# Attention scores from stacked query halves: one full-height and one half-height product in place of three half-height ones

## The chip, the cores and the metric

The kernel runs on one NeuronCore of a Trainium2 chip. Its time is the device time in microseconds (us) of one launch; a shorter time is better. The engines are TensorE (matmul), VectorE, ScalarE, GpSimd and SyncE, which issues most of the DMAs; GpSimd's queue issues some.

## What is computed

Two layers of a diffusion backbone work on 512 latent and 256 context tokens of width 1024. Each layer has a token mixer (a state-space part, a Fourier part and an attention part side by side) and a SwiGLU feed-forward part. The change is in the attention part, which has 6 heads of 64 dimensions:

```python
qg = q.reshape(B, R, GRID_W, H, d)          # 8 rows x 64 columns of latent tokens
s_win = einsum('bqhd,bwqkhd->bhqwk', q_row, k_win) * scale + bias   # 8 rows x 16 columns around
s_ctx = einsum('bqhd,bchd->bhqc', q_row, kc) * scale                # all 256 context keys
p = softmax(concatenate([s_win, s_ctx], -1))
o = p_win @ v_win + p_ctx @ vc
# na_context, in the first layer only: softmax(qc kc^T * scale) @ vc
```

## The kernel before

All matmuls keep float32 accuracy with a split: a value x is stored as hi, a rounded copy in the matmul's own 4-byte format (F32R), and lo = x - hi. A product of two such values is taken as hi*hi + hi*lo + lo*hi, three matmuls into the same PSUM tile.

Projection. `w_in` (the loop over column chunks, `CHUNKS`) makes queries and keys transposed, feature by token: chunk q0 holds heads 0 and 1, 64 rows each. `ev_q` and `ev_k` hand the chunk to `rope` (L686), which rotates it, splits it and stores hi and lo to DRAM on SyncE's queue (L708). The DRAM tensors `qd` and `kd` have for each of 384 feature rows first hi and then lo, 768 tokens each.

Attention. `attn` goes through three head pairs hp and, in each, through four latent query tiles of 128 tokens (`scores`) and in layer 0 one step for the context queries (`scores_ctx`): 15 steps in layer 0, 12 in layer 1, 27 in all. `attn_load` (L925) brings a pair's queries (L932, L937) and keys (L933) in on GpSimd's queue; the first two pairs are loaded ahead of the steps, the third during the second pair. The 128 partitions are 2 heads x 64 features. In each step `both` (L977) is called twice, for 256 window keys and for 256 context keys; a call makes for each head e three matmuls of 64 rows by 128 columns with 256 moving columns (L982): q_hi k_hi, q_hi k_lo, q_lo k_hi. Head 0 uses rows 0 to 63 of the array, head 1 rows 64 to 127, and the loop alternates the heads. Each head has a PSUM tile of 512 columns, from a pool "a" of two. VectorE then adds bias and mask and takes the row minimum (L1003), ScalarE takes the exponential, VectorE normalises (L1027), TensorE transposes the result (L1039) and multiplies by the values (L1054, and L1064 for context queries). Bias tiles come from `rbd`, which is filled by transfers of 6 x 16 rows of 1.5 KB (L923), and are combined with a mask on GpSimd (L994).

Fill. The steps are woven with other work: the Fourier part (L846, L856, L861), the gated unit (L819), and in layer 0 the modulation vectors (L161), whose weights are loaded at that time.

Order. `TileContext(schedule_with_timeline_sim=True)` is a planner that runs when the program is built. It orders each engine's instructions on its own estimate of when they become ready, so the order on TensorE need not be that of the loops. Once built, each engine works its list in order.

Pools that matter: `s` (24 buffers of 512 columns), `c` (22 of 256), `tab` (3 of 1536), `u` (one of 2816, holds the queries as `ua`).

Of the kernel before, what the change touches and what calls it, by code (L numbers as in the profile page):

```python
# [8 lines left out]
F32 = mybir.dt.float32  # L9
F32R = mybir.dt.float32r  # L10
# [8 lines left out]
NL, NC = 512, 256  # L19
NT = NL + NC  # L20
DEPTH = 2
NH, HD = 6, 64
# [12 lines left out]
class Builder:  # L35
# [60 lines left out]
    def consts(self):  # L96
        nc = self.nc
        self.cols = self.k("cols", [128, 8])
        nc.sync.dma_start(self.cols, self.ap["cols"])
        self.ident = self.k("ident", [128, 128])  # L100
        self.nidx = self.k("nidx", [128, 96])
        self.eye16 = self.k("eye16", [128, 16])
        self.junk = self.k("junk", [128, 512], mybir.dt.bfloat16)
        self.zero = self.k("zero", [1, 128], mybir.dt.bfloat16)
        nc.vector.memset(self.zero, 0.0)
        self.sgn, self.nsgn, self.sgn2pi, self.halfpi = (self.cols[:, i:i + 1] for i in range(4))
        self.mhalf = self.cols[:, 4:5]
        self.qd = [self.dram(f"qd{l}", [NH * HD, 2, NT]) for l in range(DEPTH)]
        self.kd = [self.dram(f"kd{l}", [NH * HD, 2, NT]) for l in range(DEPTH)]
        self.ud = [self.dram(f"ud{l}", [G, HC, 8, 128]) for l in range(DEPTH)]  # L110
        self.zd = [self.dram(f"zd{l}", [G, HC, 8, 96]) for l in range(DEPTH)]
        self.tabd = [self.dram(f"tabd{l}", [NU, 2, 128, 1792]) for l in range(DEPTH)]
        self.wd = [self.dram(f"wd{l}", [NU, 128, 240]) for l in range(DEPTH)]
        self.gd = [self.dram(f"gd{l}", [4, DM]) for l in range(DEPTH)]
        self.rbd = [self.dram(f"rbd{l}", [NH, 16, 8, 384]) for l in range(DEPTH)]
        self.xd = [self.dram(f"xd{l}", [6, 128, DM]) for l in range(3)]
        self.turn = [self.k(f"turn{l}", [128, 48]) for l in range(DEPTH)]
        self.rho = [self.k(f"rho{l}", [128, 48]) for l in range(DEPTH)]
        self.mcol = [[self.k(f"mc{l}{a}", [128, 2, 16]) for a in range(3)] for l in range(DEPTH)]
        self.gcol = [self.k(f"gcol{l}", [128, 2, 8]) for l in range(DEPTH)]  # L120
        self.amod = [[self.k(f"am{l}{i}", [128, 2, 8]) for i in range(2)] for l in range(DEPTH)]
        self.dcol = [self.k(f"dcol{l}", [128, NU]) for l in range(DEPTH)]
# [555 lines left out]
        self.fh[j], self.fl[j] = self.split2(eo, pc)  # L678

    def ev_q(self, l, j, pl, pc):  # L680
        self.rope(lambda i: self.qd[l][128 * j:128 * j + 128, i], pl, pc, -HD ** -0.5)

    def ev_k(self, l, j, pl, pc):
        self.rope(lambda i: self.kd[l][128 * j:128 * j + 128, i], pl, pc, 1.0)

    def rope(self, dst, pl, pc, scale):  # L686
        nc = self.nc
        if self.rc is None:
            self.rc, self.rs = self.s(), self.s()
            nc.sync.dma_start(self.rc, self.ap["rope"][:, 0, :])  # L690
            nc.sync.dma_start(self.rs, self.ap["rope"][:, 1, :])
        q, sh = self.s(), self.s()
        nc.scalar.activation(q, pl, AF.Copy, scale=scale)
        nc.vector.stream_shuffle(sh, q, [(i + 16) % 32 for i in range(32)])
        nc.gpsimd.tensor_tensor(out=sh, in0=sh, in1=self.rs, op=ALU.mult)
        self.tt(q, q, self.rc, ALU.mult)
        self.tt(q, q, sh, ALU.add)
        parts = [(q, 0, NL)]
        if pc is not None:
            qc = self.c()  # L700
            nc.scalar.activation(qc, pc, AF.Copy, scale=scale)
            parts.append((qc, NL, NT))
        for x, a, b in parts:
            new = self.s if a == 0 else self.c
            hl = (new(F32R), new(F32R))
            self.split(*hl, x)
            for i in range(2):
                nc.sync.dma_start(dst(i)[..., a:b], hl[i].bitcast(F32))  # L708


    def ssm_scan(self, l, k, tab):
# [212 lines left out]

    def attn_load(self, l, hp):  # L925

        nc = self.nc
        last = l == DEPTH - 1
        kt = self.tab(F32R, (128, 2, NT))
        rows = slice(128 * hp, 128 * hp + 128)  # L930
        ql = self.Q[hp % 2]
        nc.gpsimd.dma_start(ql, self.qd[l][rows, :, 0:NL])  # L932
        nc.gpsimd.dma_start(kt, self.kd[l][rows])  # L933
        qc = None
        if not last:
            qc = self.QC[hp % 2]
            nc.gpsimd.dma_start(qc, self.qd[l][rows, :, NL:NT])  # L937
        rb = self.z_p.tile([128, 2, 384], F32, tag="z", name="rb")
        for e in range(2):
            nc.sync.dma_start(rb[:, e, :], self.rbd[l][2 * hp + e].rearrange("c r n -> (c r) n"))  # L940
        return kt, ql, qc, rb
# [34 lines left out]

    def both(self, sp, q, k, qs, ks):  # L977

        for n, (a, b) in enumerate(((0, 0), (0, 1), (1, 0))):
            for e in range(2):  # L980
                r = slice(64 * e, 64 * e + 64)
                self.nc.tensor.matmul(sp[e], q[r, a, qs], k[r, b, ks], start=(n == 0), stop=(n == 2))  # L982

    def scores(self, l, hp, i):
        nc = self.nc
# [464 lines left out]
```

## Time and profile before

| | |
|---|---|
| median of 3 runs | 1678.88 us (1678.62 to 1682.22) |
| profiled execution | 1677.44 us |
| its span, first to last instruction | 1675.6 us |
| TensorE matmuls in flight | 1596.9 us (95%), 9097 matmuls |
| VectorE / ScalarE / GpSimd busy | 1037.3 / 608.9 / 378.8 us |
| mean granted TensorE clock | 0.977 of full speed |
| moved by DMA | 240.08 MB |

A row of the timeline merges like instructions that follow each other: start, busy time, engine, line, what is written from what, shape, count. "64*128 64x256" is a matmul that uses 64 rows and 128 columns of the array with 256 moving columns. A matmul's busy time includes its way through the array, and matmuls overlap; what one costs in a stream is the distance from its start to the next one's start. L982 is line 982 of the kernel.

### The profile page before, as it was taken

The page shows a single profiled execution, that of the slowest core. Times are in us where ns is not written, and L with a number is a line of the kernel's source. Part 1 is how long each engine was busy: PE and PEld are TensorE (multiplying, and loading weights), DVE is VectorE, ACT ScalarE, POOL GpSimd, SP SyncE. Part 2 cuts the span into 40 slices and gives each one's busy share as a digit, 9 for nine tenths or more (in the row PEclk, how much of TensorE's full clock was granted, in tenths as well). Part 3 has the DMA queues.
Part 4 walks back from the last instruction along what each step waited for, and adds up shares of the span by engine and source line. Part 5 has one row for each costly group of instructions (what it writes and reads, how often), then busy time and mean ns, then how long its engine had stood idle before and what let it go on. Part 6 is the DMA issues. An engine that isn't in the chain of part 4 may idle for free. (4 is left out here: it accounts for less than half of the span.)

```text
span 1675.6 us, 23600 instructions
## 1 busy us (share of the span) xinstructions
PE 1596.9 (95%) x9097; PEld 1311.2 (78%) x9097; DVE 1037.3 (62%) x1911; ACT 608.9 (36%) x1101; POOL 378.8 (23%) x384
## 2 busy tenths in 40 slices
PE   5988789999999999999999999999999999999997
PEld 1777676678898788878787788988778888888886
DVE  7799985774774667434434348698773634455455
ACT  5434344654627322112211127321563532222222
POOL 3367773100310323100000005276410100000002
PEclk8999799999999999999999999999899999999999
DMA  9343339662313334534423537367713322233222
GB/s 327 128 136 111 100 101 306 225 217 94 127 57 138 129 119 142 195 114 163 148 105 114 191 114 236 132 233 227 228 52 139 139 101 101 76 102 102 97 78 85
DMA packets 101391, 240.08 MB, mean 143 GB/s; under 512 B 25424, under 2 KB 56784, under 8 KB 88480
## 3 DMA queue, kind: packets, MB, share of 16 engines
q1 hardware_dynamic: 97968, 229.93, 40.3%
q0 software_dynamic: 3312, 8.65, 1.7%
q8 instruction: 71, 1.16, 0.3%
q14 instruction: 40, 0.33, 0.1%
HBM read 201.26 MB, written 38.47 MB: 143 GB/s over the span
## 5 line engine op out<-in xcount | busy, mean ns | idle before, releaser
L589 PE MATMUL b<-s,wh 128*128 128x512 f32 (+1 forms) x1856 | 553.6, 377 | 2.3 <-ACT s L580 0.8
L589 PEld LDWEIGHTS b<-s,wh 128*128 128x128 f32 x1856 | 339.9, 190 | 73.9 <-issue 10.6
L589 PE MATMUL b<-s,wl 128*128 128x512 f32 (+1 forms) x928 | 346.8, 375 | 2.5 <-DVE wl L561 2.5
L580 ACT ACTIVATE wh<-wr 128x1024 fp32r<-128x1024 f32 (+4 forms) x184 | 185.0, 1026 | 337.8 <-PE b L589 240.3
L561 DVE TENSOR_TENSOR wl<-wr,wh 128x1024 fp32r<-128x1024 f32 (+4 forms) x184 | 224.5, 1236 | 101.9 <-ACT wh L580 96.6
L278 DVE TENSOR_TENSOR q<-q,b 128x512 f32<-128x512 f32 (+1 forms) x192 | 129.2, 675 | 166.0 <-PE b L1178 165.3
L589 PEld LDWEIGHTS b<-s,wl 128*128 128x128 f32 x928 | 176.0, 190 | 33.2 <-DVE wl L561 3.8
L589 PE MATMUL b<-c,wh 128*128 128x256 f32 x944 | 183.8, 289 | 0.0
L589 PEld LDWEIGHTS b<-c,wh 128*128 128x128 f32 x944 | 154.7, 195 | 5.9 <-issue 0.6
L281 DVE SCALAR_TENSOR_TENSOR s<-s,b 128x512 f32<-128x512 f32 x88 | 60.2, 684 | 132.8 <-PE b L589 84.3
L1178 PE MATMUL b<-wh,tab 128*128 128x512 f32 x400 | 137.2, 393 | 0.1
L589 PE MATMUL b<-c,wl 128*128 128x256 f32 x472 | 134.9, 288 | 0.0
L1178 PE MATMUL b<-wh,s 128*128 128x512 f32 x384 | 129.5, 391 | 0.0
L1210 POOL TENSOR_TENSOR q<-q,g 128x512 f32<-128x512 f32 x10 | 13.8, 1380 | 361.2 <-ACT junk L515 335.5
L589 PEld LDWEIGHTS b<-c,wl 128*128 128x128 f32 x472 | 92.5, 196 | 1.7 <-issue 0.4
L1178 PEld LDWEIGHTS b<-wh,tab 128*128 128x128 f32 x400 | 75.1, 188 | 19.4 <-ACT c L1155 2.5
L1178 PEld LDWEIGHTS b<-wh,s 128*128 128x128 f32 x384 | 72.1, 188 | 19.9 <-ACT c L1155 2.5
L1178 PE MATMUL b<-wl,tab 128*128 128x512 f32 x200 | 78.3, 392 | 0.0
L1178 PE MATMUL b<-wl,s 128*128 128x512 f32 x192 | 74.6, 390 | 0.0
L527 POOL TENSOR_TENSOR ss<-ss,cols 128x1 f32<-128x1 f32 x42 | 31.0, 739 | 192.2 <-DVE ss L281 191.5
L580 ACT ACTIVATE s<-s 128x512 fp32r<-128x512 f32 x43 | 27.0, 627 | 122.0 <-DVE s L281 58.5
L452 POOL TENSOR_TENSOR u<-x,u 128x576 f32<-128x576 f32 x24 | 30.7, 1280 | 175.2 <-PE b L480 142.7
(311 smaller groups left out, 2735.8 us busy)
## 6 DMA issues: line engine op xcount, KB each, us to landing
wr<-in_w_gu SPq DMA_DIRECT2D x44, 1024.0 KB
wmod<-in_w_mod SPq DMA_DIRECT2D x46, 512.0 KB
wr<-in_w_down SPq DMA_DIRECT2D x22, 1024.0 KB
wmod<-in_w_mod SPq DMA_DIRECT2D x16, 1024.0 KB
wr<-in_w_in SPq DMA_DIRECT2D x10, 1024.0 KB
u<-in_w_mod SPq DMA_DIRECT2D x18, 512.0 KB
wr<-in_w_out SPq DMA_DIRECT2D x8, 1024.0 KB
tab<-tabd SPq DMA_DIRECT2D x12, 640.0 KB
```

What stands on the lines that cost most here:

```text
L278: self.nc.vector.tensor_tensor(out=out, in0=a, in1=b, op=op)
L281: self.nc.vector.scalar_tensor_tensor(out=out, in0=a, scalar=s, in1=b, op0=op0, op1=op1)
L452: g.tensor_tensor(out=cl, in0=v(2).unsqueeze(2).to_broadcast(sc), in1=clr.unsqueeze(3).to_broadcast(sc), op=ALU.mult)
L527: nc.gpsimd.tensor_tensor(out=ss[:, 3:4], in0=ss[:, 2:3], in1=self.mhalf, op=ALU.pow)
L561: (eng or self.nc.vector).tensor_tensor(out=lo, in0=x, in1=hi.bitcast(F32), op=ALU.subtract)
L580: ins = self.nc.scalar.activation(hi, x, AF.Copy)
L589: self.nc.tensor.matmul(out, a[k], h[k][v][:, cs], start=(k == 0 and i == 0), stop=(k == 7 and i == 2))
L1178: nc.tensor.matmul(pd, a[v][:, cs], w[:, ds], start=(j == 0 and i == 0), stop=(j == n - 1 and i == 2))
L1210: (nc.gpsimd, nc.vector)[hf].tensor_tensor(out=oo[hf], in0=oo[hf], in1=gates[t // 4][:, hf * 512:(hf + 1) * 512], op=ALU.mult)
```

## The change

- `qd` is laid out by head with 128 rows: for the even head hi rows over lo rows, for the odd head lo over hi. So a pair's query tile has for each head a column block in which 128 partitions hold hi and lo stacked. The stores are built as two blocks of 64 rows each with a stride between them.
- The key tile `kt` holds, for each head, the head's k_hi rows twice (both halves of the partitions), loaded in two DMAs, each with a stride of 0 over the two halves. k_lo goes to two more tiles, `kl`, one for the 512 latent and one for the 256 context keys, from the pools `s` and `c`.
- `both` makes for each head one matmul of 128 rows, (q_hi; q_lo) with (k_hi; k_hi), and one of 64 rows, q_hi with k_lo. The loop finishes a head before it goes to the next.

```diff
-        self.qd = [self.dram(f"qd{l}", [NH * HD, 2, NT]) for l in range(DEPTH)]
+        self.qd = [self.dram(f"qd{l}", [NH, 2 * HD, NT]) for l in range(DEPTH)]
...
     def ev_q(self, l, j, pl, pc):
-        self.rope(lambda i: self.qd[l][128 * j:128 * j + 128, i], pl, pc, -HD ** -0.5)
+
+        base = self.qd[l][2 * j]
+
+        def dst(i, a, b):
+            return bass.AP(tensor=base.tensor, offset=base.offset + i * HD * NT + a,
+                           ap=[[(3 - 2 * i) * HD * NT, 2], [NT, HD], [1, b - a]])
+        self.rope(dst, pl, pc, -HD ** -0.5)
...
-                nc.sync.dma_start(dst(i)[..., a:b], hl[i].bitcast(F32))
+                nc.sync.dma_start(dst(i, a, b), hl[i].bitcast(F32))
...
     def attn_load(self, l, hp):
...
-        nc.gpsimd.dma_start(ql, self.qd[l][rows, :, 0:NL])
-        nc.gpsimd.dma_start(kt, self.kd[l][rows])
+        qs = self.qd[l][2 * hp:2 * hp + 2].rearrange("e r n -> r e n")
+        nc.gpsimd.dma_start(ql, qs[:, :, 0:NL])
+        for e in range(2):
+            base = self.kd[l][128 * hp + 64 * e:128 * hp + 64 * e + 64]
+            nc.gpsimd.dma_start(kt[:, e, :], bass.AP(tensor=base.tensor, offset=base.offset,
+                                                    ap=[[0, 2], [2 * NT, HD], [1, NT]]))
+        kl = self.sc(F32R)
+        for x, a, b in ((kl[0], 0, NL), (kl[1], NL, NT)):
+            nc.gpsimd.dma_start(x, self.kd[l][rows, 1, a:b])
+        kt = (kt, kl)
...
-            nc.gpsimd.dma_start(qc, self.qd[l][rows, :, NL:NT])
+            nc.gpsimd.dma_start(qc, qs[:, :, NL:NT])
...
     def both(self, sp, q, k, qs, ks):
 
-        for n, (a, b) in enumerate(((0, 0), (0, 1), (1, 0))):
-            for e in range(2):
-                r = slice(64 * e, 64 * e + 64)
-                self.nc.tensor.matmul(sp[e], q[r, a, qs], k[r, b, ks], start=(n == 0), stop=(n == 2))
+        kt, kl = k
+        v, c0 = (0, ks.start) if ks.start < NL else (1, ks.start - NL)
+        for e in range(2):
+            r = slice(64 * e, 64 * e + 64)
+            self.nc.tensor.matmul(sp[e], q[:, e, qs], kt[:, e, ks], start=True, stop=False)
+            self.nc.tensor.matmul(sp[e], q[r, e, qs], kl[v][r, c0:c0 + 256], start=False, stop=True)
```

## Rows read from the trace of the kernel before

**Rows 1.** The page: TensorE's busy time, share of the span, instructions.

```profile
PE 1596.9 (95%) x9097; PEld 1311.2 (78%) x9097; DVE 1037.3 (62%) x1911; ACT 608.9 (36%) x1101; POOL 378.8 (23%) x384
```

**Rows 2.** Busy us by stretch, PEclk, DMA: scores of layers 0 and 1.

```profile
250.00:345.00 95.00, 94.46 (x746) 64.48 (x745) 61.13 (x160) 52.73 (x125) 24.11 (x36) 1.00 0.81 263
1190.00:1245.00 55.00, 51.30 (x414) 41.10 (x414) 43.05 (x119) 37.22 (x87) 12.98 (x17) 0.91 0.42 120
1198.70:1208.90 10.20, 9.27 (x46) 7.51 (x46) 7.32 (x23) 5.64 (x13) 2.20 (x3) 0.50 0.74 275
```

**Rows 3.** TensorE's waits in both stretches: who for whom, us, times, longest.

```profile
PE b L982 <- DMA u<-qd: 0.5, 1, 0.5
...
PE b L982 <- DVE am L1003: 3.1, 2, 2.0
```

**Rows 4.** The score matmuls: duration in ns, first and last start.

```profile
L982 PE MATMUL b<-tab,u x312: 274/278/579, 254.5 to 1242.0; 64*128 64x256 f32 x156
...
L982 PE MATMUL b<-tab,s x12: 276/280/384, 309.6 to 310.7; 64*128 64x256 f32 x12
```

**Rows 5.** Timeline of TensorE: runs of six and of twelve, each with its neighbours.

```profile
267.37 0.97 PE L982 MATMUL b<-tab,u 64*128 64x256 f32 x6
268.27 0.84 PE L856 MATMUL b<-s 128*1 128x256 f32 x6
...
1212.72 0.66 PE L1039 MATMUL b<-ident,q 128*128 128x128 f32 x4
1213.31 1.32 PE L982 MATMUL b<-tab,u 64*128 64x256 f32 x12
1214.56 0.43 PE L1054 MATMUL b<-q,vb 128*64 128x128 f32 x2
```

**Rows 6.** Timeline of TensorE: a run in which the heads alternate.

```profile
321.78 0.73 PE L982 MATMUL b<-tab,u 64*128 64x256 f32 x7
322.44 0.51 PE L861 MATMUL b<-wh,s 128*128 128x260 f32 x2
```

**Rows 7.** Timeline of TensorE: full-height matmuls; nine from 644.20 to 645.27.

```profile
644.20 0.28 PE L589 MATMUL b<-c,wl 128*128 128x256 f32 x1
...
645.27 0.28 PE L589 MATMUL b<-c,wl 128*128 128x256 f32 x1
```

**Rows 8.** Timeline of TensorE: single matmuls between others of another form.

```profile
326.04 0.28 PE L861 MATMUL b<-wl,c 1*128 1x260 f32 x1
326.25 0.38 PE L982 MATMUL b<-tab,u 64*128 64x256 f32 x1
326.56 0.66 PE L1039 MATMUL b<-ident,q 128*128 128x128 f32 x4
...
332.48 0.49 PE L982 MATMUL b<-tab,u 64*128 64x256 f32 x2
332.90 0.39 PE L861 MATMUL b<-wh,s 128*128 128x256 f32 x1
333.22 0.43 PE L1054 MATMUL b<-q,va 128*64 128x128 f32 x2
```

**Rows 9.** Stretches with w_in loads (46:48) and rbd transfers (50:52): PEclk, DMA share, GB/s.

```profile
46.00:48.00 2.00, 1.00 0.95 396
50.00:52.00 2.00, 0.54 0.40 151
```

**Rows 10.** Key loads on GpSimd's queue: first, last, and size with us to landing.

```profile
246.55 0.60 POOL L933 DMA_DIRECT2D tab<-kd  x1
...
1182.83 0.60 POOL L933 DMA_DIRECT2D tab<-kd  x1
...
tab<-kd POOLq DMA_DIRECT2D x6, 768.0 KB, 5.6
```

**Rows 11.** Busy us in the end of layer 0's projection, columns as in rows 2.

```profile
180.00:215.00 35.00, 28.12 (x177) 24.59 (x175) 34.83 (x55) 14.77 (x29) 24.16 (x20) 0.85 0.30 91
```

More of the change, by code (lines that the diff above doesn't have):

```diff
@@ L680, in ev_q @@
     def ev_q(self, l, j, pl, pc):
-        self.rope(lambda i: self.qd[l][128 * j:128 * j + 128, i], pl, pc, -HD ** -0.5)
+        base = self.qd[l][2 * j]
[3 more added lines that the diff above has]
+        self.rope(dst, pl, pc, -HD ** -0.5)
     def ev_k(self, l, j, pl, pc):
-        self.rope(lambda i: self.kd[l][128 * j:128 * j + 128, i], pl, pc, 1.0)
+        self.rope(lambda i, a, b: self.kd[l][128 * j:128 * j + 128, i, a:b], pl, pc, 1.0)
     def rope(self, dst, pl, pc, scale):
```

## Prediction

> **What bounds the kernel now.** I read the page first: TensorE has matmuls in flight for 1596.9 of 1675.6 us [rows 1]. The change touches the attention scores alone, so the question is what limits the two stretches in which scores are computed. The busy times by stretch [rows 2] show TensorE at 94.46 of 95 us in layer 0 and 51.30 of 55 in layer 1, against 61.13 and 43.05 for VectorE. The list of waits [rows 3] then says how often TensorE stood still there: 0.5 us for a query load in layer 0, 3.1 us for VectorE in layer 1, the latter at the start of the stretch, after which the granted clock stood at 0.50 (the lower level, 1.2 GHz) for 10.2 us [rows 2]. So both stretches go at the pace of TensorE's instruction stream, and a change of what this stream takes goes to the end of the kernel nearly in full.
>
> The lines of the score product (L982) say what is in that stream: 312 + 12 = 324 matmuls of 64 rows by 128 columns with 256 moving columns [rows 4], 12 for each of 27 steps. The durations there (278 ns) overlap and are no cost; the cost is read from start to start in the timeline of TensorE. A run of six takes 0.90 us (267.37 to 268.27) and a run of twelve 1.25 us (1213.31 to 1214.56) [rows 5].
>
> **A price list from the rows.** A full-height matmul of 256 columns among its like costs 0.12 us: 644.20 to 645.27 holds nine of them [rows 7]. A matmul alone between others of another height or width costs 0.31 us: a 64-row one from 326.25 to 326.56, a 128-row one from 332.90 to 333.22 [rows 8]. So each change between the 64-row and the 128-row form adds 0.31 - 0.12 = 0.19 us. Check: six half-height matmuls with one change ahead of them make 6 x 0.12 + 0.19 = 0.91, and the trace has 0.90 [rows 5]. Two half-height matmuls of the two heads can go side by side in one slot of 0.12: seven of them take 0.66 us at 321.78, that is 0.19 + four slots [rows 6]. But the twelve-matmul run takes 1.25 = 0.19 + nine slots, not six: one head is ahead by three matmuls, so only three pairs meet.
>
> **The change, part by part.**
>
> *Matmuls removed.* Each head and half goes from three half-height matmuls to one full-height (F) and one half-height (H): 324 become 216. At 0.12 a slot and with nothing else changed this would be a gain.
>
> *Changes of height added.* The loop now emits F, H of head 0, then F, H of head 1, so nearly every matmul changes the height. Let ' mark the second half of the keys. The planner that orders the engine's stream at build time left 14 runs of twelve; the remaining 156 matmuls I count as 26 runs of six (one head each, as 15 runs are outright). Of the 39 runs, 24 follow a full-height matmul (20 of them the transposes of L1039, as at 1212.72 [rows 5]): there F needs no change on entry, which saves 24/39 x 0.19 = 0.12 a run.
> One head alone: F H F' H' = 4 x 0.12 + 4 x 0.19 - 0.12 = 1.12 against 0.90: +0.22, times 26 = +5.7 us.
> Both heads, strictly alternating: 8 x 0.12 + 8 x 0.19 - 0.12 = 2.36 against 1.25: +1.11, times 14 = +15.5 us.
> Both heads in the manner of the runs of before, with one head ahead by three and then taking turns (F0 H0 F0' F1 H0' H1 F1' H1'): seven slots and six changes, 0.84 + 1.14 - 0.12 = 1.86: +0.61, times 14 = +8.5 us.
> The sum is +14.2 or +21.2 us. The trace can't say which order the planner writes; I take the middle, +17.7.
>
> *A rule that weighs on the same term.* The Trainium skill, "TensorE: Matmul & The Clock Gate", Part 3 on packing small matmuls, says that matmuls on different row groups start about 4 ns apart and run together. By it the old six would have cost three slots and the new two F and two H four, so +0.12 for each of 54 calls, +6.5 us with no changes of height counted. This trace shows such pairs only in part (0.66 us for seven, but nine slots for twelve), so the sum above goes by the runs as they are.
>
> *Key loads.* Each head pair's keys were one load of 768 KB on the GpSimd queue, 5.6 us from issue to landing [rows 10]. They become two loads of 384 KB, each naming the same 64 rows twice, and two loads for the low parts: three more issues per head pair, about 0.6 us each, beside a GpSimd that is 24.11 of 95 us busy [rows 2]; the mask sums (L994) queued behind them move by some 2 us. Nothing waits: later pairs load several steps ahead; cost 0. What can matter is how many DMA engines such a load gets. The transfers to rbd, whose outermost count is 6, keep the engines 0.40 busy at 151 GB/s, while 1 MB loads of 128 rows keep them 0.95 busy at 396 [rows 9]. By the same ratio a load with an outermost count of 2 would have some 2 of 16 engines and 50 GB/s: 393 KB in 7.9 us. With the 3.7 us that the old load spent besides its bytes (5.6 less 0.79 MB at 417 GB/s) that is 11.6 us after issue, the two heads beside each other. The first load of layer 0 went out at 246.55 and the first scores ran at 254.5 [rows 4, 10]; it would land at 258.2, up to 3.7 us late. In layer 1 the last key load goes out at 1182.83 [rows 10], that of the third pair, which is two pairs of steps ahead of its use; cost 0. The bounds are 0 and +3.7 for one stall, or twice that beside other traffic; I take 0, since the planner can put other ready work there, and keep +8 for the range.
>
> *Query stores.* The high part's store has an outermost count of 2 and, at the same rate, 256 KB take 5.2 us instead of below 1; 6 such and 3 of half the size, on SyncE's queue ahead of weight loads. They fall where VectorE is 34.83 of 35 us busy and TensorE is not the limit [rows 11]; I cost them at nothing. Without that cover each would delay what is behind it by up to 5 us.
>
> *Buffers.* The low keys take one 512- and one 256-column buffer per pair from pools that projections and Fourier tiles share. Before has no wait of TensorE for one [rows 3]; between 0 and a few us, taken as 0, the planner having other work.
>
> **The sum.** The profiled execution took 1677.4 us, 1.8 more than its span; 1677.4 + 17.7 = 1695.1. The median of the runs is 1.4 higher than the profiled one, so 1696.6.
>
> **The rivals.**
> *The two heights are kept apart* (the other side, faster). If the planner puts all F of a run before all H, a run of both heads has four slots of F, two of paired H and two changes: 0.72 + 0.38 - 0.12 = 0.98, -0.27 each; a lone head 0.74, -0.16. Together 14 x 0.27 + 26 x 0.16 = -8 us: 1671. For it: the planner did depart from the written order in most runs. Against: it kept three products of one head together while the other head was not ready, and F and H of a head are such a chain. It decides from two changes per run or fewer. The same time comes if the change does not do what I say, that is if H is run without a change of height; against that speak the 0.31 us of the lone ones.
> *F F H H per call.* Heads alternate within each product: six slots and four changes, 1.36, +0.11 x 14, with lone heads as above: +7 us, 1686.
> *The slower stream is hidden.* TensorE's extra time falls into waits for VectorE or loads: 1677 to 1682. Only 3.6 us of such waits exist [rows 3], so little speaks for it.
> *Late keys.* The two-engine load stalls the first scores and the clock drops after it, as it did in layer 1, where 10.2 us went at 0.50 [rows 2]: +4 to +13 on top of the forecast, 1701 to 1710. The Trainium skill, "DMA: Bandwidth & Descriptors", section on why a DMA increments its semaphore by 16, states that the count of engines is the largest up to 16 that divides the outermost sizes of both sides. The transfers to rbd agree (6 of 16 would be 0.38, and 0.40 was seen); whether GpSimd's queue does the same no row here shows.
>
> **How the numbers follow.** Alternating heights, 1691 to 1700: 0.53; the same with late keys, 1701 to 1712: 0.10; F F H H, 1683 to 1688: 0.11; heights apart, 1668 to 1675: 0.15; hidden, or small sums of both signs: 0.11. Time 1697. From 1673 to 1708 leaves out about 0.2. A measurement of this kernel tells 0.2% (3.4 us) from no change; faster by more than that 0.16, within it 0.11, slower 0.73.
>
> **What would show it.** In the changed trace, score matmuls at 0.31 us start to start where heights alternate, 0.12 where they don't; runs of eight over 1.8 us; both score stretches longer by 5 to 12 us each, with no new waits, and the rest of the kernel unmoved. Wrong would be: runs with one change of height; a first score that waits for keys; or stretches outside attention that move by more than 3 us because the planner reordered them, which no row of before can price.

## The result and the profile after

The changed kernel takes 1751.9 us (median of 5 runs, 1748.0 to 1755.0) against 1680.1 for the kernel before in the same comparison: the ratio is 1.042 (95% interval 1.040 to 1.044). The forecast was 1697, with a range from 1673 to 1708. The sign is right, the size is not: of some 72 us the forecast had 18.

The page's first row, which answers to [rows 1]: TensorE holds 108 matmuls less, and is in flight for 35 us longer.

```profile
PE 1631.7 (93%) x8989; PEld 1324.4 (76%) x8989; DVE 1033.5 (59%) x1911; ACT 611.1 (35%) x1101; POOL 392.0 (22%) x402
```

Busy time by stretch, columns as in [rows 2]: the two score stretches, and in each the 27.3 us in which the granted clock stood at 0.50, the lower of its two levels.

```profile
250.00:400.00 150.00, 124.93 (x765) 80.87 (x759) 69.19 (x181) 62.05 (x141) 29.60 (x44) 0.87 0.67 190
262.00:289.30 27.30, 11.12 (x38) 8.80 (x39) 0.69 (x1) 0.60 (x1) 7.47 (x13) 0.50 0.59 142
1248.50:1275.80 27.30, 19.64 (x59) 12.43 (x59) 11.13 (x30) 8.75 (x20) 3.40 (x4) 0.50 0.46 147
1250.00:1325.00 75.00, 68.36 (x374) 46.80 (x375) 39.77 (x110) 35.69 (x80) 13.59 (x17) 0.83 0.27 78
```

The reader is to see two things. TensorE is no longer full in layer 0 (124.93 of 150 us, where [rows 2] had 94.46 of 95), and the clock is down for a long while where before it was down for 10.2 us, in layer 1 alone. The same view, 260 to 280 us, shows how empty it was: the first two rows are before, the last two after.

```profile
260.00:270.00 10.00, 10.00 (x75) 7.63 (x71) 6.45 (x17) 4.83 (x11) 2.98 (x5) 1.00 0.89 307
270.00:280.00 10.00, 10.00 (x76) 6.42 (x77) 4.53 (x14) 4.84 (x12) 0.73 (x1) 1.00 0.73 244
...
260.00:270.00 10.00, 0.17 (x1) 0.00 (x0) 1.63 (x5) 0.80 (x2) 6.62 (x11) 0.60 1.12 269
270.00:280.00 10.00, 1.82 (x4) 1.14 (x4) 0.00 (x0) 0.00 (x0) 0.00 (x0) 0.50 0.70 161
```

TensorE's waits in the changed kernel, layer 0 (first row) and layer 1: who waits for whom, us in total, times, longest. [rows 3] had 0.5 us for a query load in layer 0.

```profile
PE b L998 <- issue: 18.0, 1, 18.0
...
PE b L998 <- DMA u<-qd: 10.7, 1, 10.7
PE b L727 <- DMA tab<-tabd: 8.8, 3, 4.3
```

The first is put down to "issue", with no releaser; it ends at 278.2, when the query load had landed (278.1 us, issued at 252.40). The third is new, too: tables of the state-space part, 1.5 us in before.

DMA issues of layer 0's attention, us to landing at the end; the first row is before, where the key load is that of [rows 10].

```profile
u<-qd POOLq DMA_DIRECT2D x3, 512.0 KB, 7.2
...
tab<-kd POOLq DMA_DIRECT2D x6, 384.0 KB, 16.1
u<-qd POOLq DMA_DIRECT2D x2, 512.0 KB, 26.1
```

And the stream itself. The first rows answer to [rows 4] (duration in ns, first and last start), the others to the twelve-run of [rows 5]: one step of both heads, strictly F H F H F H F H, 0.31 us from start to start, 2.48 us from 348.35 to 350.83.

```profile
L998 PE MATMUL b<-tab,u x104: 362/384/582, 278.2 to 1315.7; 128*128 128x256 f32 x104
...
L999 PE MATMUL b<-c,u x56: 379/382/579, 280.7 to 1316.1; 64*128 64x256 f32 x56
...
348.35 0.36 PE L998 MATMUL b<-tab,u 128*128 128x256 f32 x1
348.64 0.38 PE L999 MATMUL b<-s,u 64*128 64x256 f32 x1
348.95 0.38 PE L998 MATMUL b<-tab,u 128*128 128x256 f32 x1
...
350.52 0.38 PE L999 MATMUL b<-c,u 64*128 64x256 f32 x1
350.83 0.43 PE L1071 MATMUL b<-q,va 128*64 128x128 f32 x2
```

Where the 74.5 us between the two profiled spans lie, and those of the kernels that follow, by marks on TensorE (us from the span's start; "stream" is the time of all score matmuls from each start to the next instruction's, layers 0 and 1, waits inside a run included):

| kernel | median, ratio to before (95%) | first scores L0 | output proj. L0 | values L1 | first scores L1 | output proj. L1 | span | stream |
|---|---|---|---|---|---|---|---|---|
| before | 1680.1 | 254.5 | 353.7 | 1142.6 | 1194.6 | 1250.5 | 1675.6 | 21.5, 21.8 |
| after | 1751.9, 1.042 (1.040 to 1.044) | 278.2 | 397.7 | 1188.3 | 1255.1 | 1324.3 | 1750.1 | 38.8, 36.3 |
| x1_loads | 1728.4, 1.029 (1.027 to 1.031) | 264.9 | 375.3 | 1169.4 | 1224.8 | 1291.5 | 1716.9 | 38.6, 33.3 |
| x2_products | 1724.7, 1.026 (1.024 to 1.028) | 278.9 | 380.4 | 1174.5 | 1239.5 | 1297.7 | 1723.5 | 23.6, 23.5 |
| x3_loads_products | 1697.6, 1.010 (1.009 to 1.012) | 265.7 | 359.9 | 1151.0 | 1212.3 | 1268.5 | 1694.5 | 22.6, 21.9 |
| x9_queries_sync | 1727.9, 1.028 (1.026 to 1.030) | 256.7 | 379.4 | 1168.6 | 1231.5 | 1299.8 | 1725.5 | 37.2, 35.1 |
| x12_stores | 1734.6, 1.033 (1.031 to 1.035) | 272.5 | 387.2 | 1176.5 | 1237.5 | 1306.7 | 1732.4 | 38.0, 36.3 |
| x16_loads_stores | 1726.1, 1.027 (1.026 to 1.029) | 273.0 | 385.6 | 1177.0 | 1230.1 | 1297.2 | 1722.4 | 39.7, 33.8 |
| x14_products_only | 1719.3, 1.024 (1.022 to 1.025) | 262.3 | 380.9 | 1171.3 | 1223.8 | 1291.5 | 1717.1 | 39.2, 35.1 |
| x15_layout_only | 1695.5, 1.009 (1.008 to 1.010) | 261.8 | 368.6 | 1162.0 | 1214.0 | 1270.3 | 1696.0 | 26.8, 21.6 |
| x17_two_changes | 1691.4, 1.006 (1.004 to 1.008) | 262.4 | 369.0 | 1161.8 | 1212.3 | 1266.4 | 1691.7 | 21.6, 21.3 |
| x11_full_qsync | 1684.7, 1.003 (1.002 to 1.004) | 266.9 | 355.5 | 1148.3 | 1203.4 | 1253.5 | 1679.0 | 18.2, 17.5 |
| x19_before_loads | 1689.5, 1.006 (1.004 to 1.007) | 257.3 | 363.0 | 1155.8 | 1207.3 | 1261.9 | 1687.0 | 21.7, 20.7 |
| x18_before_pairs | 1673.3, 0.996 (0.994 to 0.997) | 255.2 | 350.9 | 1140.0 | 1192.6 | 1242.6 | 1668.4 | 16.7, 16.8 |

From after's row: 44.0 us are lost by the output projection of layer 0, of them 23.7 before the first score; 1.7 between there and the value projection of layer 1; 28.1 from there to its output projection; 0.7 after it. The rest of the kernel is unmoved. (The profiled run of x1_loads was its fastest, 9.6 under its median; its marks are to be read with that.)

### The profile page after: what moved, and what is told of

Same layout as the page of the kernel before. It is cut to its first block, busy times and chain, and to the rows that moved or that the text cites. A ratio compares the mean times of both kernels' runs of the same rounds, so it can differ in the third digit from the quotient of the medians.

```text
span 1750.1 us, 23424 instructions
## 1 busy us (share of the span) xinstructions
PE 1631.7 (93%) x8989; PEld 1324.4 (76%) x8989; DVE 1033.5 (59%) x1911; ACT 611.1 (35%) x1101; POOL 392.0 (22%) x402
## 3 DMA queue, kind: packets, MB, share of 16 engines
q0 software_dynamic: 16656, 11.06, 3.0%
## 5 line engine op out<-in xcount | busy, mean ns | idle before, releaser
L998 PE MATMUL b<-tab,u 128*128 128x256 f32 x104 | 43.2, 415 | 29.8 <-issue 18.0
```

The source lines that it names most:

```text
L998: self.nc.tensor.matmul(sp[e], q[:, e, qs], kt[:, e, ks], start=True, stop=False)
```

## The experiments

**Undoing the two suspects.** x1_loads makes the key blocks plain 64-row loads, two for each head:

```diff
-            nc.gpsimd.dma_start(kt[:, e, :], bass.AP(tensor=base.tensor, offset=base.offset,
-                                                    ap=[[0, 2], [2 * NT, HD], [1, NT]]))
+            for i in range(2):
+                nc.gpsimd.dma_start(kt[64 * i:64 * i + 64, e, :], base[:, 0, :])
```

> The changed kernel with one edit: each key block of a head is loaded into the two halves of the partitions by two plain loads of 64 rows, instead of one load that names the rows twice with a stride of 0. The bytes are the same. Theory A (two separate costs: loads on few DMA engines hold the queries behind them, and the alternation of heights costs 0.31 us a matmul): the waits of 18.0 and 10.7 us ahead of the first scores go to under 3 us, the granted clock does not fall to 0.50 in them, score matmuls still start 0.31 us apart; time 1700 to 1718. Theory B (the alternating matmuls alone, with the clock that they bring, make the loss; the loads only follow a reordered stream): the waits stay or the time they held turns up elsewhere; 1740 to 1752.

1728.4 us: 23.4 come back. That lies between the two theories: the waits go as the first one said, the time is 10 us over its range. The long waits ahead of the first scores are gone, and the loads land as the issues of layer 0 show:

```profile
tab<-kd POOLq DMA_DIRECT2D x12, 192.0 KB, 5.1
u<-qd POOLq DMA_DIRECT2D x3, 512.0 KB, 6.4
```

So the loads that read 64 rows twice over are a cause, but no more than a third of the loss. x2_products keeps the loads and goes back to six half-height products a call (the third repeats the first, so q_lo k_hi is left out):

```diff
-        for e in range(2):
-            r = slice(64 * e, 64 * e + 64)
-            self.nc.tensor.matmul(sp[e], q[:, e, qs], kt[:, e, ks], start=True, stop=False)
-            self.nc.tensor.matmul(sp[e], q[r, e, qs], kl[v][r, c0:c0 + 256], start=False, stop=True)
+        for n in range(3):
+            for e in range(2):
+                r = slice(64 * e, 64 * e + 64)
+                x = kl[v][r, c0:c0 + 256] if n == 1 else kt[r, e, ks]
+                self.nc.tensor.matmul(sp[e], q[r, e, qs], x, start=(n == 0), stop=(n == 2))
```

> The changed kernel with its loads and stores, but the products of the kernel before in kind: six half-height matmuls a call, heads alternating. The third product takes q_hi with k_hi once more, so q_lo k_hi is left out of the result. Theory A: the waits ahead of the first scores stay (over 15 us in layer 0, over 8 in layer 1), the score runs go back to 0.9 us for six and 1.25 for twelve; 1715 to 1732. Theory B: 1678 to 1690.

1724.7: the products are worth 27.2 us. The stream falls to 23.6 and 23.5 us, and the waits stay: 15.0 us in layer 0 and 10.1 in layer 1, with first scores at 278.9 and 1239.5. Two causes, then, neither of them the whole. x3_loads_products has both edits.

> The changed kernel with both of its suspects undone: the key blocks come as plain loads of 64 rows, two for each head, and the products are the six half-height ones of before (the query's low part by the keys' low is not computed, as in before). What stays of the change is the layout of the queries in DRAM with its two-row-block stores, the keys' low part in buffers of its own, and more loads per head pair. If key loads and alternation are all there is (theory A) the time is that of before within 0.3%, 1677 to 1685 us. If their two costs add up (23.4 us for the loads, 27.2 for the products out of 72 us) and something else in the layout costs the rest (theory C), it is 1695 to 1706 us, and the stage marks show where: the first scores of layer 0 later by some 10 us, or the stretch of layer 1 ahead of its scores longer by some 8. Between, 1685 to 1695, both hold in part.

(What it leaves out is q_lo k_hi, as in x2_products.) 1697.6: the costs add up (23.4 and 30.9, or 27.2 and 27.2, by the order of undoing), and 17.2 us of the 72 belong to neither. Theory C holds: first scores in layer 0 are 11.2 us late, and the value stage of layer 1 takes 45.8 us against 38.0.

**Are the queries behind the keys in their queue?** x9_queries_sync issues the two query loads of `attn_load` with `nc.sync.dma_start` in place of `nc.gpsimd.dma_start`.

> The changed kernel with its query loads issued on SyncE's queue in place of GpSimd's; key loads and products as changed. If the first scores wait because the queries are held behind the key loads in the same queue (theory A), the query load lands within 3 to 5 us of its issue, the wait of 18 us at the first scores of layer 0 falls to under 8 (what the keys themselves need, some 11.5 us after issue, is left), that of layer 1 from 10.7 to under 4, and the time is 1725 to 1742 us. If the key transfers take the memory engines from all that runs beside them (theory B), the query load lands as late as before, 20 us or more after issue, and the time stays at 1745 to 1755. If SyncE's own queue has a weight load ahead of it, the load is late by that, and the wait names it.

1727.9: 24.0 us come back with the key loads untouched. The first scores of layer 0 run at 256.7, and of the 18.0 us wait this is left:

```profile
PE b L998 <- DMA u<-qd: 3.0, 1, 3.0
```

The first theory holds, with 4.0 us left of the 10.7 in layer 1: the queries stood behind the slow key loads in one queue. The packets on that queue in the changed kernel show how. The two query loads of layer 0 have 512 packets of 2 KB; 384 of them start between 254 and 262 us, and the other 128 between 266 and 280, among the 3 KB packets of the key loads. A quarter of the queries came late, and the first score waited for it.

**The query stores.** x12_stores cuts the query stores in two of 64 rows. The edit takes every store whose outermost count is written as 2, and so the low part's as well as the high part's: 18 stores become 36, here and in all kernels with split stores.

```diff
-                nc.sync.dma_start(dst(i, a, b), hl[i].bitcast(F32))
+                d, x32 = dst(i, a, b), hl[i].bitcast(F32)
+                if d.ap[0][1] == 2:
+                    for e in range(2):
+                        nc.sync.dma_start(bass.AP(tensor=d.tensor, offset=d.offset + e * d.ap[0][0], ap=list(d.ap[1:])),
+                                          x32[64 * e:64 * e + 64])
...
```

> The changed kernel (1751.9 us) with one thing undone: each store of the queries' high part, whose outermost count is 2, becomes two stores of 64 rows. If the two-block stores hold up the table loads of the state-space stage (theory A: the wait of TensorE for them is 8.8 us in the changed kernel against 1.5 in before, and 3.0 in a kernel with split stores), this wait falls to 2 to 4 us and the time by 4 to 9 us, to 1743 to 1748. If they cost nothing, as the prediction took them (theory B), it stays at 1749 to 1756 and the wait goes elsewhere.

1734.6: 17.3 us, more than either theory had. The table wait of layer 1 behaves as the first said:

```profile
PE b L733 <- DMA tab<-tabd: 1.9, 1, 1.9
```

and the value stage there falls from 42.6 to 36.5 us. The table wait follows the stores in other kernels too: between 1100 us and 1320 us TensorE waits 5.1 to 11.5 us for these tables in the seven kernels with the stores as changed, and at most 5.7 in the nine with split ones. The wait for queries in layer 1 stays, 10.8 us. But 10.5 us of the gain lie in layer 0, where the query loads landed in 13.1 us instead of 26.1 although the last query store of that layer was issued at 202 us and the query loads at 252 and later, so the stores cannot have held them directly. Why is open: the planner gives TensorE another order of instructions in many places, so the two kernels do not differ in the stores alone.

**All transfers harmless.** x16_loads_stores has the edits of x1_loads and x12_stores, x14_products_only also that of x9_queries_sync. In x14_products_only only the alternating products and the new layout are left.

> The changed kernel with 64-row key loads and split stores, queries still behind the keys on GpSimd's queue. Theory A: with no transfer on two engines the place in the queue costs little, and the time is that of the kernel with all three undone, 1717 to 1725 us. Theory B: the queue's order costs by itself, 5 us or more: 1725 to 1735, and the first scores wait for queries in both layers.

> The changed kernel with its products as they are and its transfers made harmless: key blocks as plain 64-row loads, query loads on SyncE's queue, query stores split. What is left is the alternation of heights. By the prediction's price list in strict alternation that is +21.2 us at the full clock, and a few more where the clock stands at 0.50: theory A, 1700 to 1710 us. The rival (B) is that something of the transfers is left, more loads per head pair above all: 1710 to 1725, with the first scores of layer 0 still later than 260.

1726.1, at the lower end of its second theory's range, and 1719.3, the second one's too. In x16_loads_stores TensorE has no wait for queries left in layer 0 and one of 2.9 us in layer 1; the queries of layer 0 land in 5.9 us,

```profile
u<-qd POOLq DMA_DIRECT2D x3, 512.0 KB, 5.9
```

and their place in the queue is worth 6.8 us and no longer 24. So the three single undoings (23.4, 24.0, 17.3) overlap: together they bring 32.6, not 65. All three bring the queries of layer 0 in earlier. And 38.7 us are left, above the 21.2 of the strict alternation. x15_layout_only takes the products back as well (edit and omission as in x2_products):

> The changed kernel's layout and buffers with all transfers harmless (64-row key loads, query loads on SyncE's queue, stores split in two) and six half-height products in the order of before; the third repeats the queries' high part by the keys' high part, so that the queries' low part by the keys' high is left out. Theory A: the layout is neutral once no transfer is on two engines, 1677 to 1688 us, so that of the 1719.3 with the changed products 31 to 42 us are the products' own. Theory B: the extra loads per head pair (four for the keys in place of one, plus two) cost 10 us or more by themselves: 1690 to 1705, and the alternation is worth no more than the 21.2 us of the price list with some half-clock time.

1695.5: the products are worth 23.8 us here, and 14.4 belong to the layout with harmless transfers: the second theory's case. Most of it lies in layer 0, up to the output projection (14.9 us of the span), where TensorE is short of work and the clock drops:

```profile
260.00:270.00 10.00, 8.53 (x40) 6.75 (x34) 3.52 (x10) 2.86 (x6) 3.14 (x5) 0.66 1.04 376
270.00:280.00 10.00, 8.33 (x62) 5.65 (x61) 3.13 (x7) 1.98 (x4) 6.03 (x12) 1.00 0.88 241
```

**The number of loads.** x19_before_loads is the kernel before with its key load cut in four:

```diff
-        nc.gpsimd.dma_start(kt, self.kd[l][rows])
+        for e in range(2):
+            for i in range(2):
+                nc.gpsimd.dma_start(kt[64 * e:64 * e + 64, i, :], self.kd[l][128 * hp + 64 * e:128 * hp + 64 * e + 64, i, :])
```

> The kernel before with its one key load per head pair cut in four loads of 64 rows (high and low part of each head), on the same queue. Theory A: the number of loads is what is left of the changed layout: 1688 to 1697, with the first scores of layer 0 near 262. Theory B: the number of loads costs little, 1678 to 1686, and the 14.4 us come from the rest of the layout and the order that the planner makes of it.

1689.5: 9.1 us for nothing but three more loads per head pair. That is the first theory's time, though the first scores run at 257.3 and not near 262. In layer 0 the loads of a quarter of the size land later than the whole did (5.6 us), and TensorE runs short at 270, where it waits for modulation weights, which it did not in before:

```profile
tab<-kd POOLq DMA_DIRECT2D x12, 192.0 KB, 10.7
...
270.00:280.00 10.00, 5.86 (x34) 2.16 (x32) 3.73 (x8) 2.79 (x6) 1.19 (x2) 0.73 0.90 253
...
PE b L161 <- DMA wmod<-in_w_mod: 4.7, 2, 4.1
PE b L984 <- DMA u<-qd: 2.5, 1, 2.5
```

If that price held in x15_layout_only, some 5 us of its 14.4 would be left. That it holds there is not shown: its quarter loads land in 3.7 us, and the cause of the 14.4 was not isolated.

```profile
tab<-kd POOLq DMA_DIRECT2D x12, 192.0 KB, 3.7
```

**Is it the changes of height?** x4_loads_ffhh writes the loop as F F H H, with the loads of x1_loads:

> The plain 64-row loads of x1_loads, and in a call both heads' full-height products first, then both half-height ones. Same matmuls, other order: by the price list six slots of 0.12 and four changes of 0.19 us per step of two calls, 1.48 us in place of 2.48. Theory A (each change of height is the cost, not the full-height product): the stream keeps this order and the time is 18 to 27 us below x1_loads, 1680 to 1697. Rival C (the planner alternates them anyhow, since a head's second product stands ready): within 5 us of x1_loads.

1732.1 (ratio 1.030, 1.028 to 1.032). The planner put F H F H back in nearly every run, so the time says nothing of the order. The few steps that kept it do; this one takes 1.47 us, from 265.43 to 266.90, where the price list has 1.48:

```profile
265.43 0.48 PE L997 MATMUL b<-tab,u 128*128 128x256 f32 x2
265.84 0.38 PE L1000 MATMUL b<-s,u 64*128 64x256 f32 x2
266.16 0.50 PE L997 MATMUL b<-tab,u 128*128 128x256 f32 x2
266.59 0.38 PE L1000 MATMUL b<-c,u 64*128 64x256 f32 x2
266.90 0.51 PE L862 MATMUL b<-s 128*128 128x256 f32 x2
```

x5_loads_full makes the second product full-height too (with k_hi again: k_lo is left out), again with the loads of x1_loads; x6_full_stores is the same with split stores.

> The plain 64-row loads of x1_loads, and the second product of a head made full-height too (it takes the stacked hi keys once more, so the part with the keys' lo is left out of the result): 216 full-height matmuls, no change of height inside a run. Theory A: a step's eight matmuls take 8 x 0.12 + at most 0.19 = 0.96 to 1.15 us; 30 to 38 us below x1_loads and at or below the kernel before, 1667 to 1682. Rival C (a wait on the same PSUM tile, not the height, spaces the matmuls by 0.31): within 5 us of x1_loads.

> As the kernel with 64-row loads and two full-height products (1687.3 us), with the stores of the queries' high part split in two stores of 64 rows each, so that none has an outermost count of 2. The keys' low part is left out of the products, as there. If these stores hold SyncE's queue and with it the loads behind them in the stretch of layer 1 ahead of the scores (which was 7.8 us longer than in before), the time falls by 3 to 8 us, to 1679 to 1684. If they cost nothing, as the prediction took them, it stays at 1685 to 1690; the rival is that the residue comes from the larger number of loads per head pair on the GpSimd queue, which this kernel leaves as it is.

1687.3 (1.004, 1.003 to 1.006) and 1685.3 (1.003, 1.002 to 1.005). Without a change of height eight products take 1.03 to 1.14 us from first to next instruction instead of 2.48, and the stream of x5_loads_full 17.8 and 17.5 us. Its median is 41.2 us below x1_loads, more than the 30 to 38 expected, though 5 us over the range given for the time. A wait on the same PSUM tile, the rival, is out: the tiles are the same. Splitting the stores brings 2.0 here, within the scatter. x17_two_changes settles it with the changed kernel's own products: transfers as in x14_products_only, and the order within a step held by hand (`behind` has the planner issue one product after another), F F of the two heads, H H for both halves of the keys, F F:

```diff
...
+        full = [(sp[e], q[:, e, qs], kt[:, e, ks]) for e in range(2)]
+        half = [(sp[e], q[64 * e:64 * e + 64, e, qs], kl[v][64 * e:64 * e + 64, c0:c0 + 256]) for e in range(2)]
+        for n, x in enumerate(half + full if prev else full + half):
+            mm = lambda: self.nc.tensor.matmul(*x, start=n < 2, stop=n > 1)
+            prev = self.behind(prev, mm) if prev else mm()
+        return prev
```

> The whole computation with the changed products and harmless transfers (1719.3 us when the planner alternates the heights), and with the order of the eight products of a step held by hand: F F of the two heads, H H of both halves, F F. Two changes of height a step in place of eight, and the half-height ones of the two heads meet in one slot. By the price list a step takes 4 x 0.12 + 2 x 0.12 + 2 x 0.19 = 1.10 us against 2.48 for F H F H F H F H; 27 steps give 37 us less: theory A, 1676 to 1690 us, and the score stream near 16 us in each layer. If the cost is not in the changes of height but in these products or their operands (theory B), it stays over 1705. Runs of eight that wait for the second head's buffer could take a few us back.

1691.4, 27.9 us less than x14_products_only with the same matmuls and the same transfers. A step takes 1.21 us, from 290.97 to 292.18:

```profile
290.97 0.50 PE L1005 MATMUL b<-tab,u 128*128 128x256 f32 x2
291.40 0.39 PE L1005 MATMUL b<-s,u 64*128 64x256 f32 x2
291.63 0.28 PE L1005 MATMUL b<-c,u 64*128 64x256 f32 x2
291.84 0.50 PE L1005 MATMUL b<-tab,u 128*128 128x256 f32 x2
292.18 0.49 PE L1066 MATMUL b<-ident,q 128*128 128x128 f32 x3
```

The changes of height, then, and not the products, are what the stream pays for. The time is 1.4 over the range of the first theory: of the 37 us worked out for the stream 31.4 come back in it and 27.9 in the time, for TensorE next waits for VectorE's row minimum to free a score tile (3.8 us, layer 1) and for ScalarE's copy of the transposes (4.0 us, layer 0).

**Versions that might beat both.** x8_full_correct, x11_full_qsync and x13_full_sync compute everything with two full-height products, with a second key block (lo, hi) beside (hi, lo):

```diff
-            self.nc.tensor.matmul(sp[e], q[r, e, qs], kl[v][r, c0:c0 + 256], start=False, stop=True)
+            x = kl[2][:, e, :] if v else kl[e][:, c0:c0 + 256]
+            self.nc.tensor.matmul(sp[e], q[:, e, qs], x, start=False, stop=True)
```

> A whole computation without any change of height between the two products: the keys' block stands as (hi, lo) and a second one as (lo, hi), so that two full-height products over the stacked queries give all four terms; loads of 64 rows, query stores split in two of 64 rows. By the price list the score stretches need TensorE less than before, as in the kernel with two full-height products (17.8 and 17.5 us of score issue against 21.5 and 21.8), so 5 to 9 us are to be gained there. If the late first scores of layer 0 and the longer stretch ahead of the scores in layer 1 came from the stores (theory A), the time is 1668 to 1676 us, below before. If they come from the number of loads on the GpSimd queue, which is one more per head pair here than in the kernel with two full-height products (theory B), it is 1685 to 1700.

> The whole computation with two full-height products and no change of height between them, 64-row key loads and split stores, and now the query loads on SyncE's queue instead of behind six or eight key loads on GpSimd's. With the queries on GpSimd's queue it ran 1685.9 us: its score stretches were shorter than before's (83.4 and 49.6 us against 99.2 and 55.9 up to the output projection), but its first scores came 22.5 us later in layer 0 and the wait for queries in layer 1 was 4.6 us. If the place in the queue is the cause of the late start (theory A), the first scores of layer 0 come before 265 us and the time falls to 1665 to 1678. If the number of key loads is (theory B), it stays at 1680 to 1690.

> As the kernel with two full-height products and the query loads on SyncE's queue, with the second, swapped block of keys loaded on SyncE's queue as well, so that GpSimd issues two loads per head pair instead of eight. If GpSimd's issues one after the other delay the first scores, it is 3 to 8 us faster than that kernel. If SyncE's queue, with its weight loads ahead, takes as long, it is equal within 3 us or slower.

1685.9 (1.003, 1.002 to 1.004), 1684.7 and 1686.8 (1.003, 1.002 to 1.005): all a little over before, each the case in which the move brings nothing. The first scores do come earlier, at 277.0, 266.9 and 255.7, and the time stays, so their late start alone is not what costs here. (x13_full_sync has a new wait instead, 7.9 us for Fourier weights, which share SyncE's queue with the moved loads.) The stream of x11_full_qsync is 7.5 us shorter than before's, and it has waits for modulation weights in layer 0, where before had none, and for queries in layer 1, where before had 0.5:

```profile
PE b L161 <- DMA wmod<-in_w_mod: 9.3, 3, 8.4
...
PE b L1008 <- DMA u<-qd: 4.1, 1, 4.1
```

Whether the doubled keys hold these weights up was not tested; in the score stretch of layer 0 the DMA engines are 0.85 busy, against 0.77 in before. The cheaper way is to leave the kernel before as it is and hold its twelve half-height products of a step in pairs, by the same means as in x17_two_changes:

> The kernel before with one thing changed: the order of its twelve half-height products of a step is held by hand, the two heads taking turns through both halves, so that they meet in six slots. In before such a run takes 0.91 us from start to next, a run with one head ahead 1.25 and a run of one head alone 0.90; so 27 steps take 24.6 us where before's score stream takes 39.6 without its two waits. Theory A: the stream is the bound, as the prediction read it, and 8 to 15 us come off, 1665 to 1673. Theory B: the second head's start now holds both, and what the stream saves is lost in waits for VectorE or weight loads: 1675 to 1684.

1673.3, ratio 0.996 (0.994 to 0.997): faster than both, by 0.4% over before. The first theory nearly holds: 7.2 us come off, where it asked for 8 or more. Twelve products take 0.90 us, from 273.94 to 274.84, where [rows 5] has 1.25:

```profile
273.94 0.97 PE L982 MATMUL b<-tab,u 64*128 64x256 f32 x12
274.84 0.43 PE L1058 MATMUL b<-q,va 128*64 128x128 f32 x2
```

## Why the prediction was wrong, step by step

**What bounds the kernel: right.** The stream of TensorE sets the pace of both score stretches. It shows in both directions: x18_before_pairs saves 9.7 us of stream and 7.2 us of time, and x14_products_only spends 25.9 more than x15_layout_only and is 23.8 us slower. What was not said is how near the next waits lie: for modulation weights in layer 0 (9.3 us in x11_full_qsync).

**The price list: right.** 0.31 us where the heights alternate, 1.47 for F F H H F F H H against 1.48 worked out, 1.03 to 1.14 for eight of one height. The runs show besides how a change is paid: a step with a change on one side takes 0.20 to 0.22 us, one with a change on both sides 0.31 (x4_loads_ffhh from 265.43: 0.20, 0.21, 0.31 for the pair, 0.22, 0.21, 0.31). A run's first step has 0.2 even behind the transposes (x5_loads_full). So the order of x17_two_changes, with 1.10 in its expectation, takes 1.18 to 1.30 at the full clock.

**The alternation term: mis-sized.** The prediction had +14.2 and +21.2 us by the order that the planner would write, and took the middle, 17.7. The planner wrote the strict one, so the middle was no forecast of either case. Measured, the products are worth 23.8 us (x14_products_only to x15_layout_only), 27.2 (x2_products against after) or 30.9 (x1_loads to x3_loads_products). What goes beyond 21.2 is in part the lower clock: at 0.50 the same matmuls stand 0.51 us apart in place of 0.31, as 33 of the 216 do in the changed kernel and 35 in x14_products_only, some 7 us in each. The Trainium skill, "TensorE: Matmul & The Clock Gate", Part 3, was weighed here; its claim that matmuls on different row groups run together is borne out by this case where the order lets them meet (0.90 us for twelve in pairs).

**Key loads: this is the step that failed.** "Nothing waits: later pairs load several steps ahead; cost 0", and for layer 1 "cost 0". The landing of a key load itself was worked out well: the first one of layer 0 was issued at 242.38 and landed at 253.78, 11.4 us, where the estimate was 11.6 (the loads issued after the first two took 15.6 to 19.3). But the step asked only when the keys land, and not what stands behind them in the same queue: the query loads, 26.1 us to landing instead of 7.2 in layer 0, and TensorE waited 18.0 and 10.7 us for them. The trace of before had the warning for layer 1, where the text looked at the last key load alone: the first query load goes out behind it, at 1185.88, and lands at 1194.47, 0.1 us ahead of the first score.

```profile
1185.88 1.43 POOL L932 DMA_DIRECT2D u<-qd  x2 [2.45 <-PE b L758]
```

An idle TensorE then had its clock lowered for 27.3 us in each layer. The rival "late keys" named the mechanism and the clock, with +4 to +13 on top of the forecast; undone by 64-row loads, it was 23.4 to 27.2 (x1_loads; x2_products to x3_loads_products). The Trainium skill's rule that stood beside this rival ("DMA: Bandwidth & Descriptors", section on why a DMA increments its semaphore by 16: the count of engines is the largest up to 16 that divides the outermost sizes of both sides) agrees with this trace, now also for GpSimd's queue: from 246 to 252 us the packets of the first two key loads moved 104 GB/s together, 52 each, where the estimate for two engines was 50.

**The three more issues per head pair, at nothing: failed.** Three more loads of the same bytes cost the kernel before 9.1 us (x19_before_loads). The issues were counted (some 2 us of GpSimd), the later landing (10.7 us a piece against 5.6) and the new waits of TensorE for weights (4.7 us) and queries (2.5 in place of 0.5) were not. How the loads bring the wait for weights about is not shown.

**Query stores at nothing: failed in part.** The text said what it would cost without cover, up to 5 us for what is behind a store, and that the cover was VectorE's load in layer 0. The store's own price was about right: the packets of the store issued at 196.39 in the changed kernel start at 10 to 24 per us, 2 KB each, where the estimate of 50 GB/s has 24. But in layer 1 the tables of the state-space part are behind the stores, and TensorE waited 8.8 us for them. The 17.3 us of x12_stores are more than this explains.

**Buffers at nothing: not isolated.** No wait of TensorE is put down to one. But in layer 1 of the changed kernel GpSimd stood 8.55 us before it could load low keys into a buffer of pool `s`, until a query store, whose source lies in the same pool, had landed:

```profile
1198.47 0.54 POOL L947 DMA_DIRECT2D s<-kd  x1 [8.55 <-DMA qd<-s]
```

In x12_stores this wait is 2.2 us. The key and query loads are issued behind it in GpSimd's order; what of the late queries of layer 1 it makes was not separated.

**The rest unmoved: right,** 1.7 and 0.7 us between and after the attention parts.

**The range.** It took the bounds of each term by itself. Late queries, an idle TensorE, a lower clock and a longer stream come one after the other and in both layers; the range let each be late once. In a chain from after to before, 1751.9 less 23.4 (key loads) is 1728.4, less 30.9 (products) 1697.6, and the 17.2 that are left over before are the rest of the layout, whose causes (number of loads, stores, buffers) stay open in their shares.

## What to carry to other kernels

Count products by slots and by changes of form between neighbours in the order that is really issued; here a product less per head and half was a loss because each of the others then changed the height, and holding the order by hand was worth more than the product (27.9 us for F F H H H H F F, 7.2 for two heads in pairs). When a load gets slower, list what is queued behind it and who waits for that, and add the time at the lower clock that an idle TensorE brings with it. Here an access pattern with an outermost count of 2 was paid for by what stood behind it in the queue, and two plain loads were better than one clever one, but further loads had a price of their own as well.

## What the runs showed of the hardware that was not expected

GpSimd's queue moved 16,656 packets in the changed kernel against 3,312 in before, for 2.4 MB more. Below are its row on the page and the page's total, before first, then after.

```profile
DMA packets 101391, 240.08 MB, mean 143 GB/s; under 512 B 25424, under 2 KB 56784, under 8 KB 88480
q0 software_dynamic: 3312, 8.65, 1.7%
...
DMA packets 114609, 242.48 MB, mean 139 GB/s; under 512 B 36338, under 2 KB 68466, under 8 KB 101698
q0 software_dynamic: 16656, 11.06, 3.0%
```

Most of the increase is packets under 512 bytes: the records of this queue hold 11,280 of 4 bytes against 240. Each of the twelve key loads has 912 of them, every other load of this queue 16, in both kernels. The 64-row form of x1_loads brings the count under 512 bytes back to 25,779.

Two half-height matmuls of the two heads start 3 to 4 ns apart in x18_before_pairs when the order pairs them, six pairs in 0.90 us, so a pair costs the stream no more than one of them.

A load cut in four on GpSimd's queue landed later, not earlier (10.7 us for 192 KB, 5.6 for 768 KB), in the kernel before with nothing else changed; in x1_loads pieces of the same size took 5.1. In x15_layout_only they took 3.7. What makes the difference no run here separates.
